# Decayed attention built from the smallest blocks upwards, with keys and queries scaled in place, in a two-layer hybrid decoder

## The chip, the cores and the metric

The kernel runs on one core of one Trainium2 chip. The metric is device time in microseconds, the median of several executions; lower is better. Engine names are those of the profile: PE is TensorE (PEld its weight loads), DVE VectorE, ACT ScalarE, POOL GpSimd, SP SyncE. "L837" is line 837 of the kernel before, as printed below.

## What is computed

Two residual layers over 256 positions of 1024 features. The even layer (sparse attention) is the same in both kernels. The change is in the odd layer, gated linear attention with 4 heads of 128 key and 256 value features. Cut to what matters:

```
def gla_mix(q, k, v, log_a):          # chunks of C = 64 positions, state carried from chunk to chunk
    b = jnp.cumsum(ac, axis=2)
    inter = einsum('bhcd,bhde->bhce', qc * jnp.exp(b), state)
    diff = b[:, :, :, None, :] - b[:, :, None, :, :]
    decay = jnp.exp(jnp.where(causal[:, :, None], diff, NEG))
    att = einsum('bhid,bhjd,bhijd->bhij', qc, kc, decay)
    intra = einsum('bhij,bhje->bhie', att, vc)
    ...
def odd_layer(x, ...):
    q, k, v, g_lr, z = split(x @ w_in)
    log_a = log_sigmoid(g_lr @ gate_w2 + gate_b) / GLA_TAU          # GLA_TAU = 16
    o = gla_mix(q, k, v, log_a);  o = o * rsqrt(mean(o^2)) * gn_g * silu(z)
    return layer_norm(alpha * x + o @ w_out)
```

So query i and key j meet with a weight for each feature, the product of all decays exp(log_a) of the positions after j up to i. Both kernels compute all 256 positions without a state: a pair (i, j) belongs to the level s (1, 2, 4, ... 128) at which i and j lie in the two halves of one block of 2s positions. Then the weight splits at the middle of the block into one factor for the query and one for the key, and the level is a matmul.

## The kernel before

Dense products (helpers `denseA` and `denseB`, all recorded at L143) take each operand as the sum of a high and a low part: three matmuls for each 128 rows, 24 for a tile of 128 x 256 outputs, into one of three PSUM banks of the tag `d`. `weights(i)` brings a weight tile in two halves: SP loads it (L103), ACT casts the high part (L123), DVE or POOL subtracts to get the low part (L126, L129). A simulated timeline orders the instructions of every engine when the program is built; on the chip each engine then runs its own list in order.

The odd layer runs so: value tiles (`v_tile`, copied at L740); the gate (L747 to L770): two small matmul groups, `Abs`, `Exp` and `Ln` on ACT (L763 to L766; `Ln` needs another table than `Exp`, an ACT_TABLE_LOAD), a subtraction (L767), and four running sums `bT`, one for each head, that restart every 64 positions (L770). Then `decays(i, s)` builds, for each level, the exponents of both halves by subtracting the running sum at the block's middle (L794, L795; other lines for levels 1, 64 and 128) and takes one exponential (L796, L800, L801, L810, L791). The query and key products are copied out of PSUM by ACT (L870 into `gq`, L874 into `gk`).

`level(s, dd)` multiplies copies of keys and queries by these decays into `ma` and `mb` (L819 to L832, on DVE or POOL as the table `LEVEL_ON` says), multiplies them on PE (L846 for level 128, L851 for 64 and 32, L837 for 16 and below) and puts the result in place: ACT copies for the big levels, a masked DVE copy into 32 x 32 blocks for the small ones (L840). The levels run downwards, 128 first. Positions of chunk 0 (the first 128) are kept as [key, query] and those of chunk 1 as [query, key]; the lower half is transposed at the end (L897 to L900). The outputs of the heads follow (L921 to L924), their squares (L927), the reciprocal root (L208, L209), the scaled copy `gon` (L930), the output gate and a transpose (L938 to L952), then the output projection and the LayerNorm.

Between these groups of small matmuls stand dense products (value tiles and the gate's z tiles) that need none of them: they fill PE's time while the other engines prepare the next level.

Of the kernel before, what the change touches and what calls it, by code (L numbers as in the profile page):

```python
# [15 lines left out]
P = 128  # L16
# [9 lines left out]
# the order of the even layer's mixing: nsa and moba head pairs, moba's q, k, v tiles, gate tiles  # L26
# [4 lines left out]
# the engine (Vector or GpSimd) of each quarter of a weight tile's low parts  # L31
LO_ON = ("VVVV VVVG VVVG VGGG VGGG VGVV VVVG VVVG VVGG VVVV VVVG VGVG VVVG VVGG VVGG VVVV VVVG VVVG "
         "VGVG VGGG VVVG VVVG VGGG VVGG VGGG VGVV VGVG VVVV VVVG VVVG VVVV VVVG VVVV VVVG VGGG").split()
# and of a decay level's four operand halves
LEVEL_ON = "G--G VVVG GVVV GVVG GVGG VVVG GVGG VVVV".split()
# [9 lines left out]
def build(tc, I, out):  # L45
# [12 lines left out]
    with ExitStack() as ctx:  # L58
# [12 lines left out]
        # ---------------------------------------------------------------- exact two-part operands  # L71
# [4 lines left out]
        def cols(w, *parts):  # L76
            """(destination, source) of one half of a weight tile whose columns are the parts (first, count)"""
            def pieces(half):
                out = []
                off = 0  # L80
                for c0, n in parts:
                    out.append((lambda r, o=off, n=n: r[:, :, o:o + n], w[:, 4 * half:4 * half + 4, c0:c0 + n]))
                    off += n
                return out
            return pieces
# [46 lines left out]
        def weights(i, ahead=2):  # L132
            """the two parts of weight tile i, in halves; `ahead` further halves are split, and five more on their way"""
            top = min(2 * len(plan), 2 * i + 2 + ahead)
            while len(loaded) < top:
                while len(raws) < min(2 * len(plan), len(loaded) + 5):
                    raws.append(load_w(*divmod(len(raws), 2)))
                loaded.append(split_w(*divmod(len(loaded), 2), raws[len(loaded)]))
            return loaded[2 * i:2 * i + 2]
# [5 lines left out]
        def denseB(o, w, i, xt):  # L145
            """out[columns 128 i .., tokens]"""
# [8 lines left out]
        def denseA(o, w, c, xt):  # L155
            """out[tokens of chunk c, columns]"""
# [12 lines left out]
        def transpose_rows(src, c, xt, hs_=(0, 1), tag="t"):  # L169
            """src [128 tokens of chunk c, 1024] -> xt[:, :, chunk c], feature halves hs_"""  # L170
# [10 lines left out]
        # ---------------------------------------------------------------- inputs and constants  # L181
# [5 lines left out]
        # the tensor engine's clock comes up while the first loads are on their way  # L187
# [31 lines left out]
        class LayerNorm:  # L219
            """xv[c] <- LayerNorm(alpha xv + y), y coming in column pieces"""  # L220
# [38 lines left out]
        # ---------------------------------------------------------------- the weights in their order of use  # L259
# [38 lines left out]
        # ---------------------------------------------------------------- even layer  # L298
# [5 lines left out]
        # biases, times 8: -8 slope dist, with -BIG (and below) where the key lies ahead  # L304
# [22 lines left out]
        with tc.manual_schedule(engines={nc.tensor.engine, nc.scalar.engine, nc.vector.engine}):  # L327
            # the first tile's products follow the halves of x and of the weights as they come in
# [27 lines left out]
        # keys, selected | window: high parts on both partition halves, low parts  # L356
# [11 lines left out]
        # queries, high part of a head on its own half, low part on the other  # L368
# [11 lines left out]
        # compressed keys and values: blocks of 32 rows at a stride of 16, rows in (parity, feature) pairs  # L380
# [79 lines left out]
        # values, selected and window, and gates: [tok, chunk, sel (g d) | win (g d)]  # L460
# [10 lines left out]
        # compressed branch: scores and softmax of all heads at once, heads ordered (t, g)  # L471
# [31 lines left out]
        def softmax(pS, c, h, nb, coef):  # L503
            """pS: psum [128 q, nb, w keys]; returns P scaled by coef / sum"""
# [101 lines left out]
        # MoBA's values and queries take the place of x, which comes back for the residual  # L606
# [35 lines left out]
        # masks of 32 x 32 diagonal blocks, as [128, 32]: of level s, positions in one block of 2 s and in different  # L642
        # halves of it; above the diagonal; and the diagonal itself
# [71 lines left out]
        # ---------------------------------------------------------------- odd layer  # L715
# [3 lines left out]
        rst = op.tile([P, S], F32, name="rst")  # L719
        G.memset(rst, 1.0)  # L720
        G.memset(rst.rearrange("p (n s) -> p n s", s=64)[:, :, 0:1], 0.0)
        # the gate's second weight, its bias as row 16; twice, for the two parts of its input
# [8 lines left out]
        V.tensor_sub(gwl[:48], gw[:48], gwh[:48].bitcast(F32))  # L731
        gnh = op.tile([P, 8], F32, name="gnh")
# [13 lines left out]
        # log decay, times 16: min(u, 0) - ln(1 + exp(-|u|)), summed along each chunk of 64  # L746
        with tc.high_priority():  # L747
# [4 lines left out]
            G.tensor_scalar(gl[:32], rst[:32], 0.0, 1.0, ALU.mult, ALU.add)  # L752
# [15 lines left out]
            bT = op.tile([P, GH, S], F32, name="bT")  # L768
            for h in range(GH):
                V.tensor_tensor_scan(bT[:, h], rst, la[:, h], 0.0, ALU.mult, ALU.add)  # L770

        # causal attention with decay, level by level: above the diagonal chunk 0 as [key, query], below it
        # chunk 1 as [query, key]; the diagonal 32 x 32 blocks (of all heads) apart, side by side
# [4 lines left out]
        db = op.tile([P, NC, GH, 32], F32, name="db")  # L778

        def decays(i, s):  # L780
            if i in (1, 2):
                t = cp.tile([P, D], F32, tag="lng" if i == 1 else "lnb", name=nm("dd"))
                dd = t.rearrange("p (h t) -> p h t", h=GH)
            else:
                dd = ob.tile([P, GH, S], F32, tag="dd", name=nm("dd"))
            vw = lambda t: t.rearrange("p h (n two s) -> p (h n) two s", two=2, s=s)
            n = GH * S // (2 * s)
            b, d = vw(bT), vw(dd)
            if s == 1:
                V.tensor_sub(d[:, :, 1, :], b[:, :, 1, :], b[:, :, 0, :])  # L790
                A.activation(d[:, :, 1, :], d[:, :, 1, :], AF.Exp, scale=1.0 / TAU)  # L791
            elif s <= 32:
                ref = b[:, :, 0, s - 1:s].to_broadcast([P, n, s])
                V.tensor_sub(d[:, :, 1, :], b[:, :, 1, :], ref)  # L794
                V.tensor_sub(d[:, :, 0, :], ref, b[:, :, 0, :])  # L795
                A.activation(dd, dd, AF.Exp, scale=1.0 / TAU)  # L796
            elif s == 64:
                ref = b[:, :, 0, s - 1:s].to_broadcast([P, n, s])
                V.tensor_sub(d[:, :, 0, :], ref, b[:, :, 0, :])
                A.activation(d[:, :, 1, :], b[:, :, 1, :], AF.Exp, scale=1.0 / TAU)  # L800
                A.activation(d[:, :, 0, :], d[:, :, 0, :], AF.Exp, scale=1.0 / TAU)  # L801
            else:
                c4 = lambda t, a: t[:, :, 64 * a:64 * a + 64]
                last = lambda a: bT[:, :, 64 * a + 63:64 * a + 64].to_broadcast([P, GH, 64])
                V.tensor_sub(c4(dd, 0), last(0), c4(bT, 0))
                V.tensor_add(c4(dd, 0), c4(dd, 0), last(1))
                V.tensor_sub(c4(dd, 1), last(1), c4(bT, 1))
                V.tensor_copy(c4(dd, 2), c4(bT, 2))
                V.tensor_add(c4(dd, 3), c4(bT, 3), last(2))
                A.activation(dd, dd, AF.Exp, scale=1.0 / TAU)  # L810
            return dd

        def level(s, dd):
            on = [ENG.get(e) for e in LEVEL_ON[8 - s.bit_length()]]
            pa = bank("s")
            ma = ob.tile([P, GH, P], F32, tag="ma", name=nm("ma"))
            mb_ = ob.tile([P, GH, P], F32, tag="mb", name=nm("mb"))
            if s == 128:
                on[0].tensor_tensor(ma, gk[:, :, :P], dd[:, :, :P], ALU.mult)  # L819
                on[3].tensor_tensor(mb_, gq[:, :, P:], dd[:, :, P:], ALU.mult)  # L820
            else:
                hv = lambda t, c, two: t[:, :, c * P:(c + 1) * P].rearrange(
                    "p h (n two s) -> p h n two s", two=2, s=s)[:, :, :, two, :]
                hm = lambda t, two: hv(t, 0, two)
                on[1].tensor_tensor(hm(mb_, 1), hv(gq, 0, 1), hv(dd, 0, 1), ALU.mult)
                on[2].tensor_tensor(hm(ma, 1), hv(gq, 1, 1), hv(dd, 1, 1), ALU.mult)
                if s == 1:
                    A.copy(hm(ma, 0), hv(gk, 0, 0))
                    A.copy(hm(mb_, 0), hv(gk, 1, 0))
                else:  # L830
                    on[0].tensor_tensor(hm(ma, 0), hv(gk, 0, 0), hv(dd, 0, 0), ALU.mult)
                    on[3].tensor_tensor(hm(mb_, 0), hv(gk, 1, 0), hv(dd, 1, 0), ALU.mult)  # L832
            if s <= 16:
                for h in range(GH):
# [144 lines left out]
```

## Time and profile before

| | us |
|---|---|
| median of 3 runs (301.66 to 301.94) | 301.67 |
| span of the profiled execution, first to last instruction | 300.0 |
| PE busy | 279.0 (93%) |
| DVE busy | 221.0 (74%) |
| ACT busy | 173.7 (58%) |
| POOL busy | 125.1 (42%) |

The profile gives the span of its execution and no other time of it; the median is 1.67 us above the span. A matmul's row is longer than its turn: rows overlap, and the distance from start to start is what one costs in a stream. The odd layer's stretch from the gate to the head outputs is about 195 to 261 us.

### The profile page before, as it was taken

Reading aid. Unit: us, or ns where it says so; the run is one execution under the profiler, and the core shown is the slowest. Engines: PE = TensorE matmul, PEld = TensorE weight load, DVE = VectorE, ACT = ScalarE, POOL = GpSimd, SP = SyncE. Lnnn points to the kernel's source line nnn. Section 1 sums busy time; section 2 is a strip of 40 time slices with the busy share of each in tenths; the row PEclk is TensorE's granted clock in tenths of the full one; section 3 lists DMA queues with packets and bytes.
Section 4 is the critical chain, followed back from the end, with each engine's and each line's share of the span. In section 5 each row is a group of like instructions: output and inputs, shape, how many; then the busy total and the mean of one; then the engine's idle time right before and its main releaser. Section 6 shows DMA issues by size and latency. Waiting matters only on the chain. (4 is left out here: it accounts for less than half of the span.)

```text
span 300.0 us, 6428 instructions
## 1 busy us (share of the span) xinstructions
PE 279.0 (93%) x2392; PEld 253.6 (85%) x2392; DVE 221.0 (74%) x530; ACT 173.7 (58%) x381; POOL 125.1 (42%) x137
## 2 busy tenths in 40 slices
PE   6889999899999999999999989999885999999990
PEld 3889999788777787778999979999885999999990
DVE  6656939999766898745866995337999997484565
ACT  4589447566575767647642633668684466784011
POOL 7039419575125300020373692355078660253033
PEclk9999999999999999999999999999999599999997
DMA  7999999955442044232565283274277724000022
GB/s 212 299 322 270 339 350 294 307 171 140 100 113 72 8 133 125 64 99 70 144 203 161 61 238 123 71 213 140 74 210 227 265 72 140 4 1 2 0 72 70
DMA packets 47797, 44.84 MB, mean 149 GB/s; under 512 B 2379, under 2 KB 45429, under 8 KB 47766
## 3 DMA queue, kind: packets, MB, share of 16 engines
q1 hardware_dynamic: 47478, 43.38, 49.6%
q10 hardware_dynamic: 288, 1.05, 1.0%
q8 instruction: 19, 0.31, 0.4%
q14 instruction: 12, 0.10, 0.1%
HBM read 43.38 MB, written 1.05 MB: 148 GB/s over the span
## 5 line engine op out<-in xcount | busy, mean ns | idle before, releaser
L143 PE MATMUL d<-hi,xl 128*128 128x256 f32 (+2 forms) x304 | 87.0, 291 | 1.5 <-DVE xl L74 1.5
L143 PE MATMUL d<-hi,xh 128*128 128x256 f32 (+2 forms) x304 | 87.0, 288 | 0.0
L143 PE MATMUL d<-lo,xh 128*128 128x256 f32 (+2 forms) x304 | 86.8, 287 | 0.0
L129 POOL TENSOR_TENSOR lo<-raw,hi 128x512 fp32r<-128x512 f32 (+2 forms) x28 | 48.3, 1727 | 83.9 <-ACT hi L123 32.1
L123 ACT CAST hi<-raw 128x1024 fp32r<-128x1024 f32 (+2 forms) x60 | 62.9, 1052 | 24.2 <-PE d L143 14.3
L143 PE MATMUL d<-xh,hi 128*128 128x256 f32 x240 | 69.3, 289 | 1.1 <-DVE KL L364 1.1
L143 PE MATMUL d<-xl,hi 128*128 128x256 f32 x240 | 69.2, 289 | 0.0
L143 PE MATMUL d<-xh,lo 128*128 128x256 f32 x240 | 68.9, 288 | 0.0
L143 PEld LDWEIGHTS d<-hi,xl 128*128 128x128 f32 x304 | 57.8, 192 | 2.3 <-DVE xl L74 1.7
L143 PEld LDWEIGHTS d<-hi,xh 128*128 128x128 f32 x304 | 58.4, 192 | 0.4 <-issue 0.2
L143 PEld LDWEIGHTS d<-lo,xh 128*128 128x128 f32 x304 | 58.3, 192 | 0.5 <-issue 0.4
L143 PEld LDWEIGHTS d<-xl,hi 128*128 128x128 f32 x240 | 45.4, 189 | 2.7 <-issue 2.4
L143 PEld LDWEIGHTS d<-xh,hi 128*128 128x128 f32 x240 | 45.3, 189 | 2.7 <-issue 1.5
L143 PEld LDWEIGHTS d<-xh,lo 128*128 128x128 f32 x240 | 45.5, 190 | 1.2 <-issue 0.8
L129 DVE TENSOR_TENSOR lo<-raw,hi 128x512 fp32r<-128x512 f32 (+2 forms) x38 | 32.7, 869 | 14.0 <-ACT hi L123 11.8
L126 DVE TENSOR_TENSOR lo<-raw,hi 128x1024 fp32r<-128x1024 f32 (+1 forms) x27 | 35.5, 1316 | 7.2 <-ACT hi L123 7.2
L126 POOL TENSOR_TENSOR lo<-raw,hi 128x1024 fp32r<-128x1024 f32 (+2 forms) x10 | 24.6, 2460 | 16.7 <-ACT hi L123 16.7
L512 ACT ACTIVATE pr<-ng,sm 128x128 f32<-128x128 f32 (+1 forms) x48 | 21.6, 453 | 2.8 <-DVE sm L510 2.1
L518 DVE TENSOR_SCALAR pr<-pr,sm 128x128 f32<-128x128 f32 (+1 forms) x48 | 18.5, 415 | 0.4
L510 DVE CUSTOM_DVE_ANT_0 ng<-s,b 128x128 f32<-128x128 f32 (+1 forms) x48 | 15.7, 350 | 2.4 <-PE s L531 1.6
L514 DVE RECIPROCAL sm<-sm 128x2 f32<-128x2 f32 (+1 forms) x32 | 5.2, 162 | 12.4 <-ACT pr L512 12.1
L121 ACT CAST hi<-raw 128x512 fp32r<-128x512 f32 x20 | 11.6, 618 | 4.0 <-DMA raw<-ev_w_in 2.1
(251 smaller groups left out, 450.5 us busy)
## 6 DMA issues: line engine op xcount, KB each, us to landing
raw<-ev_w_in SPq DMA_DIRECT2D x18, 512.0 KB, 6.0
raw<-od_w_in SPq DMA_DIRECT2D x16, 512.0 KB, 4.1
raw<-ev_w_in SPq DMA_DIRECT2D x18, 256.0 KB, 5.3
raw<-od_w_in SPq DMA_DIRECT2D x8, 520.0 KB, 3.8
raw<-od_w_out SPq DMA_DIRECT2D x8, 512.0 KB, 3.5
raw<-ev_w_out SPq DMA_DIRECT2D x8, 256.0 KB, 4.0
raw<-ev_w_out SPq DMA_DIRECT2D x4, 512.0 KB, 3.5
x<-x SPq DMA_DIRECT2D x4, 256.0 KB, 3.0
```

What stands on the lines that cost most here:

```text
L121: A.copy(h_, r_)
L123: A.copy(hv, rv)
L126: ENG[on[0]].tensor_sub(lv, rv, hv.bitcast(F32))
L129: ENG[e].tensor_sub(l_, r_, h_.bitcast(F32))
L143: T.matmul(o, a, b, start=(j == 0), stop=(j == len(terms) - 1))
L510: V.tensor_tensor_reduce(ng[:, b, :w], pS[:, b], b8[:, h, S - w:], -0.125, 3e38, ALU.add, ALU.min, sm[:, 0, b:b + 1])
L512: A.activation(pr[:, b, :w], ng[:, b, :w], AF.Exp, bias=sm[:, 0, b:b + 1], scale=-1.0, accum_out=sm[:, 1, b:b + 1])
L514: V.reciprocal(sm[:, 2, :nb], sm[:, 1, :nb])
L518: V.tensor_scalar(pr[:, b, :w], pr[:, b, :w], sm[:, 2, b:b + 1], None, ALU.mult)
```

## The change

The running sums, the table `LEVEL_ON`, `decays` and the copies `mb` go. One exponential makes the decay of every single position, `TT`. `decay(s)` is the decay of a whole block of s positions; POOL multiplies neighbours to get it from level to level (six products, 512 columns down to 16). Keys and queries lie in one tile `KQ` and are multiplied in place on DVE (`grow`): going to level s, the keys of the left half-blocks take the decay of the right half-block behind them, and the queries of the right half-blocks that of the left one. The levels run upwards, 1 to 128. For levels up to 16 ACT gathers the matmul's weights (`ma`, two copies a level) and the other operand is read from `KQ` with a stride; from 32 on both are slices of `KQ`, and level 32 is 16 matmuls of 32 columns in place of 8 of 64. `gq` moves from a tile of its own into a third use of the tag `dd`, which has two buffers, after `la` and `ab`. The two small-block steps (transpose and masked copy into `db`) come after level 16, the transpose of `attL` after level 64.

```diff
-            bT = op.tile([P, GH, S], F32, name="bT")
-            for h in range(GH):
-                V.tensor_tensor_scan(bT[:, h], rst, la[:, h], 0.0, ALU.mult, ALU.add)
+            TT = op.tile([P, 2 * GH * S], F32, name="TT")
+            A.activation(TT[:, :GH * S], la.rearrange("p h t -> p (h t)"), AF.Exp, scale=1.0 / TAU)
+        def decay(s):
+            o, n = 2 * (GH * S - GH * S // s), GH * S // s
+            return TT[:, o:o + n]
...
+        KQ = op.tile([P, 2, GH, S], F32, name="KQ")
+        gq = ob.tile([P, GH, S], F32, tag="dd", name="gq")
+        def halves_of(s, h, at):
+            low, up = KQ[:, 0, h, P + at:], KQ[:, 1, h, at:]
+            dims = [[2 * s, 16 // s], [up.offset - low.offset + s, 2], [1, s]]
+            return bass.AP(low.tensor, low.offset, [list(low.ap[0])] + [d for d in dims if d[1] > 1])
+        def grow(s, heads=slice(0, GH)):
+            r = s // 2
+            if s > 1:
+                d, m = decay(r), decay(s).rearrange("p (h n) -> p h n", h=GH)[:, heads]
+                d = d.rearrange("p (h n two) -> p h n two", h=GH, two=2)[:, heads]
+                if s < 128:
+                    G.tensor_tensor(m, d[:, :, :, 0], d[:, :, :, 1], ALU.mult)
+            if s == 128:
+                k, q = KQ[:, 0, heads, :64], KQ[:, 1, heads, P + 64:]
+                V.tensor_tensor(k, k, d[:, :, 0, 1:2].to_broadcast([P, GH, 64]), ALU.mult)
+                V.tensor_tensor(q, q, d[:, :, 1, 0:1].to_broadcast([P, GH, 64]), ALU.mult)
+                return
+            k, q = (KQ[:, i, heads].rearrange("p h (n two s) -> p (h n) two s", two=2, s=r)[:, :, i] for i in range(2))
+            n = k.shape[1]
+            d = d.rearrange("p h n two -> p (h n) two")
+            V.tensor_tensor(k, k, d[:, :, 1:2].to_broadcast([P, n, r]), ALU.mult)
+            V.tensor_tensor(q, q, d[:, :, 0:1].to_broadcast([P, n, r]), ALU.mult)
...
             if s <= 16:
+                ma = ob.tile([P, GH, P], F32, tag="ma", name=nm("ma"))
+                A.copy(half(ma, 0), half(KQ[:, 0, :, :P], 0))
+                A.copy(half(ma, 1), half(KQ[:, 1, :, P:], 1))
...
-                A.copy(gk[:, 2 * j + i], pd[:, :S])
+                A.copy(KQ[:, 0, 2 * j + i], pd[:, :S])
...
-        for i, s in enumerate(steps):
-            level(s, dds[i])
+        for s in [1 << li for li in range(8)]:
+            if s > 1:
+                grow(s)
+            level(s)
```

The built order moves at two places that the prediction speaks of (line numbers of the changed kernel differ by a few). The first is ACT's list at the gate, the place of the query copies `gq` and of the key copies (`gk` before, `KQ` now); `d_...` is the PSUM tile that a copy empties. Before:

```order
L870 ACTIVATE gq<-d_2720 128x256
L763 ACTIVATE ab<-s_2633 128x512
L763 ACTIVATE ab<-s_2640 128x512
L765 ACTIVATE ab<-ab 128x1024
L874 COPY gk<-d_2746 128x256
L123 CAST hi_2814<-raw_2683 128x1024
L766 ACT_TABLE_LOAD
L766 ACTIVATE ab<-ab 128x1024
L123 CAST hi_2821<-raw_2689 128x1024
L874 COPY gk<-d_2785 128x256
```

and now:

```order
L858 COPY KQ<-d_2724 128x256
L760 ACTIVATE ab<-s_2632 128x512
L760 ACTIVATE ab<-s_2639 128x512
L762 ACTIVATE ab<-ab 128x1024
L121 CAST hi_2792<-raw_2660 128x1024
L763 ACT_TABLE_LOAD
L763 ACTIVATE ab<-ab 128x1024
L121 CAST hi_2799<-raw_2666 128x1024
L858 COPY KQ<-d_2763 128x256
L767 ACT_TABLE_LOAD
L767 ACTIVATE TT<-la 128x1024
L851 ACTIVATE gq<-d_2659 128x256
```

Both query copies of the first two heads stood before `Abs` and now stand behind `TT`'s exponential; the first key copy moved ahead of `Abs`. The second place is PE's list at the last levels and the head outputs. Before, from the outputs of the first two heads of chunk 0 on:

```order
L921 MATMUL o_3295<-VV,att_2656 128x256 x2
L921 MATMUL s_3296<-VV,att_2656 128x256 x2
L923 MATMUL s_3315<-VV,att_2658 128x256
L924 MATMUL s_3315<-VV,att_2657 128x256
L923 MATMUL s_3315<-VV,att_2658 128x256
L924 MATMUL s_3315<-VV,att_2657 128x256
L143 MATMUL d_3511<-hi_3429,xh_2128 128x256
```

and now, from the last matmuls of level 64 on:

```order
L838 MATMUL s_3104<-KQ 64x64 x8
L906 MATMUL o_3256<-VV,att_2652 128x256 x2
L885 MATMUL t_3115<-ident,attL 128x128 x4
L830 MATMUL s_3123<-KQ 128x128 x4
L906 MATMUL s_3257<-VV,att_2652 128x256 x2
L908 MATMUL s_3276<-VV,att_2654 128x256
L909 MATMUL s_3276<-VV,att_2653 128x256
...
L909 MATMUL o_3277<-VV,att_2653 128x256
L932 MATMUL t_3344<-ident,gon 128x128 x2
L141 MATMUL d_3605<-hi_3475,xh_2128 128x256
```

On SP the two loads of the odd layer's LayerNorm (L216) now stand before the weight loads of the last value tile, about 35 us of the program earlier; their buffers held two of the `dd` tiles before. Levels 64 and 128 and the transpose of `attL` now stand next to the outputs with no dense product between them, and the 35 dense products that stood between the third and the fourth pair of outputs are gone from there.

## Rows read from the trace of the kernel before

**Rows 1.** The page's busy time, share of the span and instructions.

```profile
PE 279.0 (93%) x2392; PEld 253.6 (85%) x2392; DVE 221.0 (74%) x530; ACT 173.7 (58%) x381; POOL 125.1 (42%) x137
```

**Rows 2.** PE's waits from 200 to 265 us: total, times, longest.

```profile
PE s L851 <- DVE mb L832: 4.0, 1, 4.0
PE s L883 <- ACT gk L874: 1.1, 1, 1.1
PE s L851 <- DVE db L885: 0.9, 1, 0.9
```

**Rows 3.** Windows (start:end length, PE, PEld, DVE, ACT, POOL busy, PEclk, DMA share, GB/s).

```profile
206.00:250.00 44.00, 38.07 (x512) 36.64 (x511) 43.02 (x60) 26.46 (x42) 24.59 (x18) 0.92 0.57 173
...
229.02:233.00 3.98, 0.00 (x0) 0.03 (x1) 3.98 (x7) 3.48 (x6) 2.28 (x2) 0.88 0.71 227
233.00:238.90 5.90, 5.90 (x68) 5.72 (x69) 5.80 (x9) 3.29 (x7) 4.54 (x4) 0.50 0.82 274
```

**Rows 4.** Chain that ended last, in order of time, before PE's long stop ends.

```profile
226.20 1.70 DVE dd L794
...
229.05 1.67 DVE lo L126
230.72 1.13 DVE lo L129
```

**Rows 5.** Groups by line, 203 to 252 us: busy us, mean ns, idle before.

```profile
L796 ACT ACTIVATE dd<-dd 128x1024 f32<-128x1024 f32 x5 | 5.3, 1058 | 10.4 <-DVE dd L795 10.4
...
L770 DVE TENSOR_TENSOR_SCAN bT<-rst,la 128x256 f32<-128x256 f32 x4 | 4.6, 1205 | 0.0
L794 DVE TENSOR_TENSOR dd<-bT 128x512 f32<-128x512 f32 x5 | 4.5, 902 | 0.1
L795 DVE TENSOR_TENSOR dd<-bT 128x512 f32<-128x512 f32 x5 | 4.0, 791 | 0.0
```

**Rows 6.** DVE and POOL in order of time: the same work alone and beside POOL.

```profile
214.37 0.68 DVE L794 TENSOR_TENSOR dd<-bT 128x512 f32<-128x512 f32 x1
...
226.12 1.77 DVE L794 TENSOR_TENSOR dd<-bT 128x512 f32<-128x512 f32 x1
...
219.68 1.45 POOL L819 TENSOR_TENSOR ma<-gk,dd 128x512 f32<-128x512 f32 x1 [9.38 <-ACT dd L810]
```

**Rows 7.** PE in order of time: dense products after the gate's, and two small levels.

```profile
198.56 0.39 PE L143 MATMUL d<-xh,lo 128*128 128x256 f32 x1
198.79 0.28 PE L143 MATMUL d<-xh,hi 128*128 128x256 f32 x1
198.91 0.27 PE L143 MATMUL d<-xl,hi 128*128 128x256 f32 x1
...
240.74 0.76 PE L837 MATMUL s<-mb,ma 128*32 128x32 f32 x64
241.43 0.39 PE L143 MATMUL d<-hi,xl 128*128 128x256 f32 x1
```

**Rows 8.** ACT in order of time, the second key copy behind `Ln` and a cast.

```profile
204.79 0.36 ACT L874 COPY gk<-d 128x256 f32<-128x256 f32 x1
```

**Rows 9.** ACT at the head outputs of chunk 0.

```profile
254.40 0.39 ACT L927 ACTIVATE sq<-s 128x256 bf16<-128x256 f32 x1
...
256.74 0.84 ACT L930 ACTIVATE gon<-o,rs 128x256 f32<-128x256 f32 x2 [0.67 <-POOL rs L209]
```

**Rows 10.** PE's stream at the head outputs.

```profile
252.97 0.59 PE L923 MATMUL s<-VV,att 128*128 128x256 f32 x2
253.40 0.59 PE L924 MATMUL s<-VV,att 128*128 128x256 f32 x2
```

**Rows 11.** Windows at the end of the span (columns of rows 3).

```profile
292.25:300.00 7.75, 0.00 (x0) 0.00 (x0) 4.64 (x10) 0.91 (x2) 2.40 (x4) 0.80 0.20 68
295.00:300.00 5.00, 0.00 (x0) 0.00 (x0) 2.10 (x4) 0.00 (x0) 1.03 (x2) 0.69 0.31 105
```

**Rows 12.** SP's issue of the odd layer's LayerNorm scale.

```profile
224.97 0.50 SPq L216 DMA_DIRECT2D lng<-od_ln_g  x1
```

More of the change, by code (lines that the diff above doesn't have):

```diff
@@ L33 @@
          "VGVG VGGG VVVG VVVG VGGG VVGG VGGG VGVV VGVG VVVV VVVG VVVG VVVV VVVG VVVV VVVG VGGG").split()
-LEVEL_ON = "G--G VVVG GVVV GVVG GVGG VVVG GVGG VVVV".split()
 BANKS = {'d': 3, 's': 2, 't': 2, 'o': 1}
@@ L717, in build @@
         ob = pool("ob", 2, reuse_waits="tile")
-        rst = op.tile([P, S], F32, name="rst")
-        G.memset(rst, 1.0)
-        G.memset(rst.rearrange("p (n s) -> p n s", s=64)[:, :, 0:1], 0.0)
         gw = ob.tile([P, 512], F32, tag="ma", name="gw")
@@ L731, in build @@
         V.tensor_sub(gwl[:48], gw[:48], gwh[:48].bitcast(F32))
+        ones = op.tile([32, S], F32, name="ones")
+        G.memset(ones, 1.0)
         gnh = op.tile([P, 8], F32, name="gnh")
@@ L751, in build @@
             gl = ob.tile([P, S], F32R, tag="tho", bufs=4, name="gl")
-            G.tensor_scalar(gl[:32], rst[:32], 0.0, 1.0, ALU.mult, ALU.add)
+            G.tensor_scalar(gl[:32], ones[:32], 0.0, 1.0, ALU.mult, ALU.add)
             A.copy(gl[:16], pt[:16, :S])
@@ L778, in build @@
         db = op.tile([P, NC, GH, 32], F32, name="db")
[L780 to L811, printed above, removed]
@@ L813, in level @@
-        def level(s, dd):
-            on = [ENG.get(e) for e in LEVEL_ON[8 - s.bit_length()]]
-            pa = bank("s")
[L816 to L832, printed above, removed]
+        KQ = op.tile([P, 2, GH, S], F32, name="KQ")
@@ L833, in level @@
+        def level(s):
+            pa = bank("s")
             if s <= 16:
+                ma = ob.tile([P, GH, P], F32, tag="ma", name=nm("ma"))
+                half = lambda t, two: t.rearrange("p h (n two s) -> p h n two s", two=2, s=s)[:, :, :, two, :]
+                A.copy(half(ma, 0), half(KQ[:, 0, :, :P], 0))
+                A.copy(half(ma, 1), half(KQ[:, 1, :, P:], 1))
                 for h in range(GH):
@@ L836, in level @@
                         js = slice(32 * j, 32 * j + 32)
-                        T.matmul(pa[js, 32 * h:32 * h + 32], ma[:, h, js], mb_[:, h, js], start=True, stop=True,
-                                 tile_position=(0, 32 * j))
+                        T.matmul(pa[js, 32 * h:32 * h + 32], ma[:, h, js], halves_of(s, h, 32 * j),
+                                 start=True, stop=True, tile_position=(0, 32 * j))
                 li = s.bit_length() - 1
@@ L845, in level @@
                 if s == 128:
-                    T.matmul(pv[:, h], ma[:, h], mb_[:, h], start=True, stop=True)
+                    T.matmul(pv[:, h], KQ[:, 0, h, :P], KQ[:, 1, h, P:], start=True, stop=True)
                     continue
-                for a in (0, 64):
-                    rows, other = slice(a, a + 64), (64 - a if s == 64 else a)
-                    cols_ = slice(other, other + 64)
-                    T.matmul(pv[rows, h, cols_], ma[:, h, rows], mb_[:, h, cols_], start=True, stop=True,
-                             tile_position=(0, a))
+                for a in range(0, P, s):
+                    rows, other = slice(a, a + s), (a - s if a // s % 2 else a + s)
+                    cs = slice(other, other + s)
+                    ma, mb_ = KQ[:, 0, h, rows], KQ[:, 1, h, cs]
+                    if a > other:
+                        ma, mb_ = KQ[:, 1, h, P + a:P + a + s], KQ[:, 0, h, P + other:P + other + s]
+                    T.matmul(pv[rows, h, cs], ma, mb_, start=True, stop=True, tile_position=(0, a))
             if s == 128:
@@ L859, in level @@
                 A.copy(attL[up, :, lo_], pv[up, :, lo_])
-        steps = [1 << li for li in range(7, -1, -1)]
-        dds = [decays(i, steps[i]) for i in range(4)]
-        gq = op.tile([P, GH, S], F32, name="gq")
-        gk = op.tile([P, GH, S], F32, name="gk")
         for j in range(2):
@@ L870, in build @@
                 A.activation(gq[:, 2 * j + i], pd[:, :S], AF.Copy, scale=float(P) ** -0.5)
+            hs = slice(2 * j, 2 * j + 2)
+            V.tensor_tensor(KQ[:, 1, hs].rearrange("p h t -> p (h t)"), gq[:, hs].rearrange("p h t -> p (h t)"),
+                            decay(1)[:, 2 * j * S:(2 * j + 2) * S], ALU.mult)
             for i in range(2):
@@ L882, in build @@
                     o = (c * GH + h) * 32
-                    T.matmul(pa[js, o:o + 32], gk[:, h, cs], gq[:, h, cs], start=True, stop=True,
+                    T.matmul(pa[js, o:o + 32], KQ[:, 0, h, cs], gq[:, h, cs], start=True, stop=True,
                              tile_position=(0, 32 * j))
@@ L889, in build @@
         G.memset(blocks[:, 0], 0.0)
-        for i, s in enumerate(steps):
-            level(s, dds[i])
-            if len(dds) < 8 and i + 1 < 8:
-                dds.append(decays(len(dds), steps[len(dds)]))
-            if s == 32:
+        for s in [1 << li for li in range(8)]:
+            if s > 1:
+                grow(s)
+            level(s)
+            if s == 16:
+                V.transpose(blocks[:, 1].rearrange("p h q -> p (h q)"), blocks[:, 0].rearrange("p h q -> p (h q)"))
+                V.copy_predicated(db.rearrange("p c h q -> p (c h) q"), upper[:, None, :].to_broadcast([P, 8, 32]),
+                                  blocks.rearrange("p c h q -> p (c h) q"))
+            if s == 64:
                 pt = bank("t")
@@ L898, in build @@
                 A.copy(attc[1], pt.rearrange("p (h q) -> p h q", h=GH))
-        V.transpose(blocks[:, 1].rearrange("p h q -> p (h q)"), blocks[:, 0].rearrange("p h q -> p (h q)"))
-        V.copy_predicated(db.rearrange("p c h q -> p (c h) q"), upper[:, None, :].to_broadcast([P, 8, 32]),
-                          blocks.rearrange("p c h q -> p (c h) q"))
         for c in range(NC):
@@ L966 @@
     from concourse.bass_utils import run_bass_kernel_spmd
-    nc = bacc.Bacc("TRN2", target_bir_lowering=False, num_devices=1)
+    nc = bacc.Bacc("TRN2", target_bir_lowering=False, num_devices=1,
+                  dynamic_dma_scratch_size=1024)
     arrays, I = {}, {}
```

## The prediction

> **What bounds the kernel now.** I read the busy times first: PE 93%, DVE 74%, ACT 58%, POOL 42% [rows 1]. PE's stream is the bound, so a change is worth what it takes out of PE's idle or slow time, less what it puts in. The changed part has next to no PE work of its own: two small levels together, 32 matmuls, take 241.43 - 240.74 = 0.69 us [rows 7].
>
> Next I read PE's waits in that stretch: three, 4.0, 1.1 and 0.9 us [rows 2]. All other work of the stretch is covered by the dense products. The long one is level 32's second operand, late from DVE. The chain says why: ahead of its multiplications DVE's list has the subtractions of a later level (1.70 us) and the low parts of weights (1.67 and 1.13 us) [rows 4]. DVE is busy 43.02 of 44.00 us from 206 to 250 [rows 3]; there DVE, not PE, sets the pace. And in that long stop the granted clock falls from 2.4 to 1.2 GHz: the mean is 0.88 over the stop, 0.50 over the 5.90 us after it, in which PE is busy throughout [rows 3]. Half of 5.90 us, 2.95, is lost to that.
>
> So the ledger of before: waits 6.0, slow clock 2.95. A dense product's row lasts 0.28 us but its turn is 198.91 - 198.79 = 0.12 [rows 7], so each wait, counted from the end of a row, is 0.16 short: 0.5 more. Together **9.4 us** lie between PE's work and a stream without gaps. After PE's last product at 292.25 comes a tail of 7.75 us [rows 11], LayerNorm and stores, which the change leaves alone.
>
> **The change, part by part.** *Sums, subtractions, exponentials.* On DVE the scans (4.6 us) and ten subtractions (4.5 and 4.0 us) go [rows 5], with smaller ones and 15 multiplications on top that I don't count. In come 16 multiplications, 14 over 512 columns. The nearest row has the same shape, with a broadcast operand, at 0.68 us alone [rows 6]: at most 16 x 0.68 = 10.9 us. Beside a running POOL instruction that same row took 1.77. So the multiplications cost 0.68 to 1.77 each. I take 0.68, because POOL's list shrinks too: 13 multiplications go, and six products come, of which the largest is 1.45 us by the row of equal width [rows 6] and each further one is half as wide, some 2.9 together. On ACT five exponentials of 1.06 go (5.3 us) [rows 5] and four others; one comes, and ten gathers `ma`, for which the copy of equal size gives 0.36 [rows 8]. They run beside dense products; were that cover gone, each level would cost two multiplications, two copies and their hops, over 2 us.
>
> The Trainium skill ("GPSIMD Engine Reference", Specifications) says that POOL's SBUF interfaces are shared with DVE and that DVE instructions with two SBUF inputs contend for them. By that rule the multiplications stay near 0.68 only as long as POOL is idle; the rows at 0.68 and 1.77 agree.
>
> *The waits of before.* DVE no longer prepares levels ahead of need; each level needs two multiplications and, up to 16, two ACT copies after the last level's matmuls. Between two small levels the order puts 37 to 46 dense products, 4.4 to 5.5 us. DVE's work in one such interval is two multiplications (1.4), two low parts of weights (1.13 to 1.67 each [rows 4]) and under 1 us of small things: 4.3 to 5. It fits, barely. I let all 9.4 us go. Level 32 as 16 narrow matmuls costs as much as 16 small ones, 0.35 us: 0 to 0.3 gained, I take 0.
>
> *What is late next: the bank at the gate.* `gq` waits for a buffer that the gate's `la` holds until the new exponential has read it. So the first two query products sit in two of the three PSUM banks, and the key products pass one after the other through the third. The second key product starts about where dense products resume, 198.56, and takes 24 x 0.12: done at 201.4 [rows 7]. The next needs the same bank, after the second key copy on ACT, which stands behind `Abs`, `Exp`, a cast, the table load, `Ln` and another cast, as before. There it started at 204.79 [rows 8]; with the first copy moved ahead it ends at 204.8 to 205.15, I take 204.9. PE stops for **3.5 us** where before it never did. Queued behind it are all further dense products, so nothing covers it. Behind that copy on ACT wait the table load and `TT`, which gate the multiplications; the first level comes some 120 dense products later, 14 us, so they have room.
>
> *The last levels.* Levels 64 and 128 and the outputs now follow each other without dense products. (a) The outputs wait for ACT's copy of level 64: 0.36 by the copy of equal width [rows 8] and two hops, 0.4 to 0.9, I take 0.6. (b) Chunk 1's last two heads need the bank of chunk 0's first two. From the third square to the end of the first two scaled copies is 254.40 to 257.58 = 3.2 us [rows 9]; meanwhile PE has four matmuls of 253.40 - 252.97 = 0.43 each [rows 10], 1.7. With a hop of 0.2: 1.7 idle (1 to 2.5). (c) The same chain runs for chunk 1, with two more scaled copies (0.84), a cast (about 1.05), a tanh and the split of the transposed block (0.7): 5.8 us, against 30 dense products (3.6) and six transposes (0.7): 1.5, with a hop 1.6 (0.5 to 2.5). Before, 35 dense products lay between and hid all this. Sum **3.9 us**.
>
> *The rest.* The LayerNorm loads, 0.50 us of SP each [rows 12], move ahead of weight loads on SP; DMA has a share of 0.57 in the stretch they leave [rows 3] and every weight tile is loaded several halves ahead: nothing. If that cover were gone, a late weight tile would stop PE for about one load's time on the queue.
>
> **Sum.** Gone 9.4, new 3.5 + 3.9 = 7.4: 2.0 us less. The profiled span is 300.0; the median of the runs is 301.67, so 1.67 us lie around the span, which I leave as they are. 301.67 - 2.0 = **299.7**.
>
> **Rivals.** *The clock falls in the new stop.* In the long stop of before it fell about 3.06 us after PE's last row: mean 0.88 over 3.98 us means 0.95 us at half [rows 3]. At the end of the span it held longer: a mean of 0.69 over the last 5 us means 3.1 us at half, a fall at 296.9, 4.65 us after PE's end [rows 11]. A stop of 3.5 lies between the two. If it falls, PE resumes at half speed: between 1.5 and 2.95 us lost; I take 2.0: **301.7**, no change.
>
> The Trainium skill ("TensorE: Matmul & The Clock Gate", Part 1) has the low clock as the state without activity, into which a long enough pause falls back; by it this change moves that loss rather than removes it. The fall at 232 us agrees.
>
> *DVE sets the pace of the levels (the slower side).* If the multiplications in place meet POOL as often as not, they take (0.68 + 1.77) / 2 = 1.2 us [rows 6]; one interval is then 2.4 + 2.8 + 0.8 = 6.0 us on DVE against 5.0 of dense products, and each of the four levels 2 to 16 makes PE wait about 1 us: 299.7 + 4 = **303.7**. It decides from about 0.7 to 0.95 us for a multiplication on, as the interval has 5.0 or 5.5 us of dense products. For it: DVE is the fuller engine now; strided in-place operands have no row. Against: POOL has only a few low parts left there.
>
> *The change doesn't do what it says.* DVE's long wait came partly from weights' low parts [rows 4], which stay. If they alone hold the levels back, the 4.0 us wait stays and the new stops come on top: **303.7**, down to 301.7 where half of it overlaps with them.
>
> *Gain without the stop.* If the second key copy comes earlier than the list says: 3.5 less, **296.2**.
>
> **Chances.** Forecast without a fall of the clock 0.46, with it 0.36, DVE's pace 0.09, no effect 0.06, no stop 0.03. About 0.2%, 0.6 us, is what a measurement can tell: faster is below 301.07, slower above 302.27. The forecast lies below but for its bounds (0.43 faster, 0.03 same); the fallen clock gives 0.08 faster, 0.19 same, 0.09 slower; DVE's pace is slower; no effect 0.02 same, 0.04 slower; no stop is faster. Faster 0.54, same 0.24, slower 0.22. The forecast's own range, from the bounds of the stops, is 298.6 to 300.9; with the fallen clock 302.6 is reached.
>
> **What would show it.** Right: PE without a wait on DVE in the levels; one PE stop near 201 to 205 us released by ACT's key copy; short ones at level 64, at the outputs of chunk 1's last heads and before the output projection; DVE well under 43 us busy in 206 to 250; multiplications near 0.68. Wrong: PE waits on DVE at each level, multiplications over 1 us, or a clock of 0.50 after the new stop.

## The result and the profile after

The changed kernel takes 304.39 us (median of 5, 302.59 to 305.22) against 301.66 for the kernel before: a ratio of 1.0089, 95% interval 1.0064 to 1.0114. In a second comparison (e0 below) the medians are 302.76 and 301.21, ratio 1.0057, 1.0035 to 1.0078. So it is slower by 1.5 to 2.7 us; the forecast was 2.0 us faster, and 304.39 lies above the range.

The profiled execution is the fastest of the first five: 302.59 us, span 300.9. Its page, busy times and granted clock in 40 slices:

```profile
PE 278.7 (93%) x2408; PEld 252.0 (84%) x2408; DVE 208.6 (69%) x510; ACT 171.2 (57%) x381; POOL 112.6 (37%) x129
PEclk9799999999999999999999999999999999999996
```

DVE has lost 12.4 us and POOL 12.5 against [rows 1], PE next to nothing, and the slow stretch in the middle is gone: in this execution the change does what it says. Windows of the same trace, the levels and the new stop at the gate (columns of rows 3):

```profile
206.00:250.00 44.00, 44.00 (x589) 42.74 (x589) 31.14 (x41) 26.02 (x46) 12.00 (x11) 1.00 0.52 157
201.01:204.54 3.53, 0.28 (x3) 0.07 (x2) 1.85 (x3) 3.50 (x5) 1.75 (x1) 1.00 0.36 77
```

In the 44 us in which PE was busy for 38.07 at a mean clock of 0.92 [rows 3] it is now busy throughout at full clock, and DVE is down from 43.02 to 31.14. What came instead are PE's waits from 190 to 301 us, in total, times, longest:

```profile
PE d L141 <- ACT KQ L858: 3.3, 1, 3.3
PE o L908 <- ACT gon L915: 1.8, 1, 1.8
PE t L932 <- DVE gon L927: 1.2, 1, 1.2
PE d L141 <- DVE xl L936: 0.9, 1, 0.9
PE o L906 <- ACT att L844: 0.5, 1, 0.5
PE d L141 <- ACT xh L934: 0.2, 1, 0.2
```

The three waits of [rows 2] are gone, and none of the six is on DVE in the levels or on a load. The first is the bank stop at the gate, the fifth is (a), the second (b), and the third, fourth and sixth together are (c). ACT in order of time at the gate shows the first as the prediction's list had it: the key copy (L858) comes behind the table load, the logarithm (`Ln`, L763 here) and a cast, and ends at 204.48; PE goes on at 204.54.

```profile
200.93 1.28 ACT L763 ACT_TABLE_LOAD   x1
202.23 1.06 ACT L763 ACTIVATE ab<-ab 128x1024 f32<-128x1024 f32 x1
203.19 1.03 ACT L121 CAST hi<-raw 128x1024 fp32r<-128x1024 f32 x1
204.12 0.36 ACT L858 COPY KQ<-d 128x256 f32<-128x256 f32 x1
```

**A measure without the noise of the start.** The four traces of the changed kernel differ by 1.14 us in when they reach the odd layer's gate, where the kernels are still the same. I therefore compare from the second of the last two transposes into `x1t` to the last dense product. PE's rows that bound it, in the kernel before (the second transpose starts 0.10 after the row):

```profile
185.14 0.38 PE L175 MATMUL t<-ident,x 128*128 128x128 f32 x2
...
291.97 0.28 PE L143 MATMUL d<-hi,xl 128*128 128x256 f32 x1
```

and in the changed kernel:

```profile
184.96 0.38 PE L173 MATMUL t<-ident,x 128*128 128x128 f32 x2
...
292.45 0.28 PE L141 MATMUL d<-hi,xl 128*128 128x256 f32 x1
```

| us | that stretch | of it PE's stops, start to start less a turn of 0.12 | from the last product's start to the end |
|---|---|---|---|
| before, three traces (e4) | 106.72, 106.70, 106.71 | 6.3 | 8.0 |
| changed, profile and e0 | 107.38, 107.38 | 8.8 | 8.4 |
| changed, e6 and e8 | 108.72, 108.91 | 8.8 | 8.4 |
| e1, buffer of its own | 104.47 | 5.9 | 8.4 |
| e2, stop filled | 108.04 | 6.1 | 8.4 |
| e3, levels first | 103.91 | 5.3 | 8.4 |
| e5, tail covered | 102.79 | 4.3 | 8.4 |
| e7, last low parts on DVE | 101.68 | 3.1 | 8.7 |

Traces of one kernel with the same clock agree within 0.03 us, so a difference of 0.1 us counts here. Each edited kernel has one trace.

### The profile page after: what moved, and what is told of

It is laid out like the page before. It is cut to its first block, busy times and chain, and to the rows that moved or that the text cites. A ratio compares the mean times of both kernels' runs of the same rounds, so it can differ in the third digit from the quotient of the medians.

```text
span 300.9 us, 6426 instructions
## 1 busy us (share of the span) xinstructions
PE 278.7 (93%) x2408; PEld 252.0 (84%) x2408; DVE 208.6 (69%) x510; ACT 171.2 (57%) x381; POOL 112.6 (37%) x129
## 4 chain that ended last, share of the span: by engine, by line
PE 71%; DVE 6%; ACT 3%; issue 1%; POOL 1%; DVEq 0%; ACTq 0%; POOLq 0%
PE d L141 52%; PE t L535 2%; PE s L529 2%; PE o L580 2%; PE s L565 2%; DVE gon L927 1%; PE o L551 1%; PE o L541 1%; PE t L572 1%; PE o L546 1%; PE s L528 1%; PE s L564 1%; DVE lo L124 1%; DVE x L254 1%; DVE x L245 1%
## 5 line engine op out<-in xcount | busy, mean ns | idle before, releaser
L127 POOL TENSOR_TENSOR lo<-raw,hi 128x512 fp32r<-128x512 f32 (+2 forms) x28 | 47.6, 1702 | 109.2 <-ACT hi L121 57.7
L141 PE MATMUL d<-hi,xl 128*128 128x256 f32 (+2 forms) x304 | 85.9, 287 | 2.3 <-DVE xl L72 1.5
L141 PE MATMUL d<-lo,xh 128*128 128x256 f32 (+2 forms) x304 | 85.9, 284 | 0.0
L141 PEld LDWEIGHTS d<-hi,xl 128*128 128x128 f32 x304 | 56.8, 189 | 3.3 <-DVE xl L72 1.7
L141 PEld LDWEIGHTS d<-hi,xh 128*128 128x128 f32 x304 | 57.5, 189 | 1.0 <-ACT xh L934 0.5
L141 PEld LDWEIGHTS d<-lo,xh 128*128 128x128 f32 x304 | 57.5, 189 | 0.4 <-issue 0.4
L127 DVE TENSOR_TENSOR lo<-raw,hi 128x512 fp32r<-128x512 f32 (+2 forms) x38 | 31.1, 830 | 16.6 <-ACT hi L121 14.7
L124 DVE TENSOR_TENSOR lo<-raw,hi 128x1024 fp32r<-128x1024 f32 (+1 forms) x27 | 33.8, 1256 | 11.6 <-ACT hi L121 11.5
L512 DVE RECIPROCAL sm<-sm 128x2 f32<-128x2 f32 (+1 forms) x32 | 5.1, 161 | 12.4 <-ACT pr L510 12.2
```

What stands on the lines that cost most here:

```text
L124: ENG[on[0]].tensor_sub(lv, rv, hv.bitcast(F32))
L127: ENG[e].tensor_sub(l_, r_, h_.bitcast(F32))
L141: T.matmul(o, a, b, start=(j == 0), stop=(j == len(terms) - 1))
```

## The experiments

Theory A stood first: the new stops weigh as much as what went, and in many executions the clock falls in one of them as well. Its rivals have letters in the expectations.

**e0, the change once more.**

> The changed kernel once more, unedited, beside the kernel before. Theory A (PE's new stops, 8.8 us in the trace, stand where 9.0 us of waits and slow clock stood; in most executions the clock also falls in or behind one of the new stops): times between 302.5 and 305.5 us, the longer ones with the lower mean clock of TensorE, and a profile taken in a longer one shows a stretch at 0.50 behind the stop at 201 to 205 us. Theory B (the clock has no part in it; the new levels themselves vary): longer executions at the same mean clock.

302.76 us (8 executions, 302.05 to 304.32), before 301.21. The trace repeats the first one wait by wait. Its execution was again the fastest, and the clock does not fall at its stop. Of the mean clocks, the two lowest (0.980, 0.981) belong to the two longest times (304.32, 304.18), but among the others 303.73 has 0.985 and 302.05 has 0.984: a sign for theory A, no proof. Open until e6.

**e1, `gq` in a buffer of its own.**

```diff
-        gq = ob.tile([P, GH, S], F32, tag="dd", name="gq")
+        gq = op.tile([P, GH, S], F32, name="gq")
```

> The changed kernel with one edit: the raw query copies (gq) get a buffer of their own, so that they no longer wait for the one the gate holds. Theory A: the stop of about 3.5 us at 201 to 205 us is gone, and with it the place where the clock can fall: 302.6 - 3.5 = 299.1 us, 298.7 to 299.8, all executions close together, and faster than the kernel before. Rival C (the stop only hides other waits: what the gate's chain holds up comes later, in the levels): PE then waits on DVE or ACT at the first levels, 302 us or more. Rival D (the clock falls in the stops at the end, not at the gate): times still spread by 1.5 to 2.6 us, 299 to 302.

299.54 us (299.15 to 300.45), ratio to before 0.9937 (0.9917 to 0.9956): faster than before. PE's waits, those that replace the first line above:

```profile
PE o L908 <- ACT gon L915: 1.8, 1, 1.8
...
PE s L867 <- ACT KQ L858: 0.4, 1, 0.4
```

The stop of 3.4 is gone, one of 0.5 at the diagonal blocks takes its place, and the stretch is 2.91 shorter: one shared buffer decides the sign of the whole change. Rival C, which wanted 302 us or more, falls. The times spread by 1.3 us, as those of the kernel before do (300.69 to 302.45), so they don't separate A from D.

**e2, the stop filled with matmuls.**

```diff
+                if j == 0 and i == 1:
+                    pw2 = bank("o")
+                    for _ in range(28):
+                        T.matmul(pw2[:, :S], x1t[0][:, 0, :P], x1t[0][:, 0], start=True, stop=True)
```

> The changed kernel with 28 more matmuls of 128 x 256 into an unused PSUM bank, placed after the second key product, where PE stops; their product is not used. They take 28 x 0.12 = 3.4 us, about as long as the stop, so the stop stays as long but PE runs in it. Theory A: the clock cannot fall at the gate any more while all waits stay: 302.6 to 303.2 us, executions within 0.6 us of each other. Rival D (the clock falls in the stops at the end): 302.6 to 305.2 as without the filling. Theory B: the same, 304.4.

303.41 us (302.52 to 304.04): inconclusive; the narrow 302.6 to 303.2 of theory A did not come. The 28 matmuls and what was left of the wait (0.7) came to 0.66 more than the stop, and the executions still spread by 1.5 us, though the mean clock was 0.990 to 0.994 in five of six. The spread is then not the clock's alone.

**e3, the levels ahead of the weights' preparation** (on top of e1).

```diff
-            if s > 1:
-                grow(s)
-            level(s)
+            with tc.high_priority():
+                if s > 1:
+                    grow(s)
+                level(s)
```

> The edit of e1, and the multiplications and matmuls of all levels get priority over the weights' preparation in the order of the work. If the multiplications are late anywhere (rival E: DVE's list sets the pace of the levels), 1 us or more below e1, 298 or less. Theory A: only the short wait after level 64, up to 0.6 us: 298.5 to 299.1.

299.04 us (298.89 to 299.36). The stretch is 0.56 below e1: stop (a), 0.59, and nothing else. DVE's list does not set the pace of the levels; rival E falls, and with it the prediction's rival of that name.

**e4, the kernel before, two more traces.**

> The kernel before, unedited, for its trace. The prediction counted 2.95 us of slow clock (a half-speed stretch at 232 to 239 us) as lost in it. Theory F (the clock falls there in only some executions, or for a shorter stretch, so the change can't win back 2.95 in the median): from the last transpose ahead of the gate, 185.24 in the first trace, to the last product it takes less than the first trace's 106.7 us, down to 104.0 without a fall. Rival G (it falls in every execution): 106.7 again, with a half-speed stretch of about 6.8 us.

> The kernel before once more, for a third trace: theory F 104.0 to 106.2 us from that transpose to the last product, rival G 106.7.

Rival G holds: the clock falls in both, and the stretch is the same to 0.03 us. Window behind the long stop of the first:

```profile
233.29:239.28 5.99, 5.99 (x68) 5.81 (x69) 5.89 (x9) 3.30 (x7) 4.56 (x4) 0.50 0.78 263
```

So what the change removes is lost in all three traces of before.

**e5, cover for the tail** (on top of e3): the last two z tiles wait in PE's list for the outputs. The lines that fill `last`, which keeps the last matmul of each group, are left out here.

```diff
-                denseA(pd[:, :256], weights(i_gz[j]), c, x1t)
+                wz, at = weights(i_gz[j]), {(3, 0): ('o', 0), (3, 1): ('o', 1)}.get((j, c))
+                with tc.issue_after(last[at].ins) if at else nullcontext():
+                    denseA(pd[:, :256], wz, c, x1t)
```

> The edit of e3, and the last two tiles of dense products (48 matmuls, 5.8 us) are issued only behind the output matmuls of chunk 0 and of chunk 1, so that they lie beside the chain of squares, scalings and products that ends the attention. Theory A (the stops of 5.2 us at the end stand there because the levels have used up the dense products): about 1 us below e3, as the one of 2.2 us goes, a wait of 0.9 comes at level 128, whose cover is taken away, and the last two, ahead of the output projection, stay: 297.5 to 298.3. Rival H (ACT's chain sets the end, whatever PE has to do): as e3, 298.8 to 299.3.

297.99 us (297.36 to 298.40), ratio to before 0.9882 (0.9861 to 0.9903). PE's waits:

```profile
PE t L937 <- DVE gon L932: 1.2, 1, 1.2
PE s L832 <- DVE KQ L803: 0.9, 1, 0.9
PE d L141 <- DVE xl L941: 0.9, 1, 0.9
PE s L869 <- ACT KQ L860: 0.4, 1, 0.4
PE d L141 <- ACT xh L939: 0.2, 1, 0.2
```

As theory A had it, and not rival H: (b) is gone, level 128 waits for the multiplications that the held products covered, and (c) stays as it was. The dense products are a stock: what the levels use up is missing at the end.

**e6 and e8, the change for a third and a fourth trace.**

> The changed kernel, unedited, for another trace. Theory A: where its time is above 303.5, a half-speed stretch stands behind the stop at the gate or at the outputs, and the stretch from the last transpose ahead of the gate to the last product is 108.5 us or more. Theory B: that stretch is 107.4 as in both traces so far, and what differs lies ahead of 185 us, where this kernel and the one before are the same.

> The changed kernel, unedited, for a fourth trace: 107.4 us from the last transpose ahead of the gate to the last product if the clock holds in the stop at the gate, 108.7 with a half-speed stretch of 3.4 us from about 204 us on if it falls.

304.0 and 304.67 us. In both, the clock falls at the gate, in e6 just before PE goes on and in e8 just after. Windows of e6, the stop and what follows:

```profile
201.08:204.61 3.53, 0.28 (x3) 0.08 (x1) 1.85 (x3) 3.50 (x5) 1.76 (x1) 0.95 0.30 72
204.61:207.68 3.07, 3.06 (x14) 3.06 (x15) 1.31 (x3) 2.86 (x4) 0.67 (x1) 0.50 0.61 175
```

and of e8:

```profile
201.57:205.10 3.53, 0.28 (x3) 0.07 (x1) 1.85 (x3) 3.50 (x5) 1.75 (x1) 1.00 0.29 69
205.10:208.69 3.59, 3.59 (x17) 3.59 (x18) 1.83 (x3) 2.85 (x4) 1.12 (x2) 0.52 0.72 213
```

Dense turns at the low clock, from e6's PE in order of time:

```profile
205.21 0.41 PE L141 MATMUL d<-xh,lo 128*128 128x256 f32 x1
205.42 0.41 PE L141 MATMUL d<-xh,hi 128*128 128x256 f32 x1
205.63 0.41 PE L141 MATMUL d<-xl,hi 128*128 128x256 f32 x1
```

A turn is 0.21 us here and 0.12 at full clock [rows 7]. The same stop of 3.53 us left the clock at 1.00 in the first trace and in e0. The fall costs 1.34 us in e6 and 1.53 in e8 (108.72 and 108.91 less 107.38): in two of four traces the new stop brings back half of what the old one cost. Theory B falls for these two.

The 15 executions of the changed kernel, these two included, fall into two groups by their mean clock. Seven at 0.981 or less took 304.0 to 305.2 us, with a median of 304.39; eight at 0.984 or more took 302.1 to 304.1, with a median of 302.67. The two traces with a fall are in the first group (0.979 and 0.974), the two without in the second (0.985 and 0.984). So the clock probably fell in about half of the executions, in three of the first five and in two of the eight of e0. The mean also holds the start of the program, so this is a sign and not a count.

**e7, the last low parts on DVE** (on top of e5). In the changed kernel's trace (c) is 2.7 us long, and DVE and POOL stand there like this:

```profile
265.63 2.17 DVE L927 TENSOR_TENSOR gon<-gon,tho 128x256 f32<-128x256 f32 x3
...
268.16 2.16 DVE L927 TENSOR_TENSOR gon<-gon,tho 128x256 f32<-128x256 f32 x1
```

```profile
265.04 1.80 POOL L127 TENSOR_TENSOR lo<-raw,hi 128x512 fp32r<-128x512 f32 x1 [0.44 <-ACT hi L121]
267.44 2.60 POOL L124 TENSOR_TENSOR lo<-raw,hi 128x1024 fp32r<-128x1024 f32 x1 [0.60 <-ACT hi L121]
```

The last multiplication ends at 270.32, right behind POOL's instruction, which ends at 270.04. Three quarters of the last weight's low parts are POOL's by the table `LO_ON`, whose last entry is the edit:

```diff
-         "VGVG VGGG VVVG VVVG VGGG VVGG VGGG VGVV VGVG VVVV VVVG VVVG VVVV VVVG VVVV VVVG VGGG").split()
+         "VGVG VGGG VVVG VVVG VGGG VVGG VGGG VGVV VGVG VVVV VVVG VVVG VVVV VVVG VVVV VVVG VVVV").split()
```

> The edit of e5, and the low parts of the last weight (the output projection's) are all made on DVE; before, POOL made three quarters of them. Theory J (in the stops ahead of the output projection DVE's multiplication of gon waits for POOL's instruction: 2.2 us instead of 0.42 beside it): each such multiplication takes 0.42 again, the stops of 2.8 us there shrink to about 1.8, and the kernel is 1.0 us below e5, 297.0 (296.6 to 297.5). Rival K (the two low parts of 1.2 us that now stand on DVE in the same chain cost what the shorter multiplications give): as e5, 297.7 to 298.3, or 0.5 above.

297.55 us (296.52 to 297.63) against 301.62 in its comparison, ratio 0.9866 (0.9846 to 0.9885). The same instruction, and the low part that DVE now makes itself:

```profile
262.25 0.42 DVE L932 TENSOR_TENSOR gon<-gon,tho 128x256 f32<-128x256 f32 x1
262.73 1.23 DVE L124 TENSOR_TENSOR lo<-raw,hi 128x1024 fp32r<-128x1024 f32 x1
```

PE's waits:

```profile
PE s L832 <- DVE KQ L803: 0.9, 1, 0.9
PE t L937 <- DVE gon L932: 0.7, 1, 0.7
PE d L141 <- ACT xh L939: 0.6, 1, 0.6
PE s L869 <- ACT KQ L860: 0.4, 1, 0.4
```

The three multiplications ahead of this last one fall from 2.17 us together to 1.09. The stops of (c) fall from 2.8 in e5 to 1.6 us and the stretch by 1.11. Against the kernels before of their own comparisons e5 is 3.1 us ahead and e7 4.1. Theory J holds. This version beats both kernels.

## Why the prediction was wrong

The sum was "gone 9.4, new 7.4: 2.0 us less". Without a fall of the clock the traces give: the stretch +0.67 and its end +0.42, 1.1 us more. With a fall, 2.4 to 2.6 more. The 3.1 us between -2.0 and +1.1, step by step:

- **Gone, 9.4.** The waits were right: 6.3 measured, 6.5 in the sum. The slow clock was priced at half of 5.90 us, 2.95. In e6 and e8 3.07 and 3.59 us of slow busy time cost 1.34 and 1.53, 0.43 to 0.44 for each; by that, 5.90 us cost an estimated 2.6. It is less than half because the turn at full clock is 0.12 and not half of 0.21. Gone: 8.9. Short by 0.5.
- **The bank at the gate, 3.5.** Right in place, cause and size: 3.4, released by the copy that was named.
- **(a), 0.6, and (b), 1.7.** 0.6, and 2.05, which is 0.35 over the 1.7 taken and inside its bounds of 1 to 2.5.
- **(c), 1.6: the failed term.** It measured 2.7. The chain as listed had squares, scaled copies, a cast, a tanh and a split; DVE's two steps between the tanh and the split, the second of them the multiplication of `gon` by the gate, were not in it. The last multiplication took 2.16 us instead of 0.42, held beside POOL; e7 shows what that cost: the same stops come to 1.6 without POOL. That this equals the 1.6 of the sum is in part luck, as the list was two links short. The prediction had read this very mechanism from [rows 6], and had weighed it only for the multiplications of the levels. There it did strike now and then, but had cover. DVE's groups, 206 to 250 us:

```profile
L808 DVE TENSOR_TENSOR KQ<-KQ,TT 128x512 f32<-128x512 f32 x6 | 6.4, 1059 | 1.3 <-PE s L838 1.3
L809 DVE TENSOR_TENSOR KQ<-KQ,TT 128x512 f32<-128x512 f32 x6 | 4.1, 680 | 0.0
```

  0.68 as taken for the second of each pair, a mean of 1.06 for the first: three of these six took 1.12 to 1.59, each beside a POOL subtraction of 1.80, and the other three 0.68 to 0.69. With DVE busy for 31 of 44 us, none of it reached PE.
- **The rest, 0.** 0.8 us more in the stretch and 0.4 behind the last product. Adding up PE's starts by kind, an estimated 0.3 of the 0.8 stands at the levels (5.8 us with their edges before, the half-speed stretch taken out, 6.1 now), 0.3 at the matmuls of the outputs, and the rest is not placed. The small levels stood in pairs, 0.69 for two [rows 7]; now most stand alone, and that costs more:

```profile
226.04 0.28 PE L141 MATMUL d<-lo,xh 128*128 128x260 f32 x1
226.25 0.46 PE L821 MATMUL s<-KQ,ma 128*32 128x32 f32 x32
226.64 0.39 PE L141 MATMUL d<-hi,xl 128*128 128x260 f32 x1
226.87 0.28 PE L141 MATMUL d<-hi,xh 128*128 128x260 f32 x1
```

  One level takes 0.39 from its first matmul to the next dense product, and the dense turns ahead of it and behind it last 0.21 and 0.23 instead of 0.12, as they do at a pair. Each pair that is split thus costs 0.1 more inside and 0.2 more at its edges. For the outputs no row names a cause. The 0.4 lies behind the last DVE instruction (297.10 to the end at 299.98 before, 297.59 to 300.87 now). The prediction had said that the change leaves this tail alone. The stores are not later: SP has seen the last one 2.0 us behind that instruction in both traces, and the 0.4 comes after that, in the closing instructions of the program. Why stays open.

0.5 - 0.1 + 0.35 + 1.1 + 0.8 + 0.4 = 3.05. The range had its own fault: the bounds of the four stops, added up, give 297.6 to 301.9 and not 298.6 to 300.9.

**The rivals.** "The clock falls in the new stop" had 0.36 and was priced at 2.0; it came in two of four traces at 1.3 to 1.5. With the measured sum it makes the difference between a kernel that is 1.1 us slower and one that is 2.5 slower. By the mean clocks most of the first five executions had it and most of the eight of e0 had not, which fits the 1.6 us between the two medians. Because the sum itself was 3.1 too low, the range, which reached to 302.6 by this rival alone, did not hold. "DVE sets the pace" and "the change doesn't do what it says" did not happen. "Gain without the stop" (296.2) was the right question with the wrong sum: e1, which takes away just that, gives 299.5.

The Trainium skill ("SBUF — State Buffer", section "SBUF: two separate sides") calls what DVE and POOL share an exclusive lock, which a DVE instruction with two SBUF inputs or a POOL instruction that reads SBUF holds for its whole length while the other blocks. The 2.16 us against 0.42, and an end 0.28 us behind POOL's, agree. The prediction had weighed the contention of the two only for the levels, where the change adds work.

## What to carry to other kernels

Work that covers waits is a stock: when a change empties a stall in the middle, count where the same dense products are missing afterwards, at the end above all. Before giving a tile to a shared tag, follow who still holds its buffers; here that one line cost a stop of 3.4 us, 2.9 of it net, and sometimes the clock. List every link of a chain that has lost its cover, and price each as it runs beside POOL or DVE, not alone. Count the groups into which a change splits PE's small matmuls, for each has two edges.

## What was not expected of the hardware

- The same stop of PE, 3.53 us to the hundredth, was followed by 1.2 GHz in two traces and by 2.4 GHz in two others. A forecast has to give such a loss a chance, not a yes or no.
- A DVE multiplication of 128x256 that meets a POOL subtraction of 2.60 us takes five times as long as alone and ends 0.28 us behind it; a mean of the two prices, as the prediction's rival took, describes neither case.
- A half-speed stretch cost 0.43 to 0.44 us for each microsecond, not 0.5: 0.21 us a turn against 0.12.
